# The second half's sum over partitions moved into the first group of direct products, and its squares added from the fourth chunk on

## The chip, the cores and the metric

One NeuronCore of a Trainium2 chip runs the whole program. The metric is device time in microseconds (us), the median of the runs; lower is better. PE is the matmul engine (TensorE), DVE is VectorE, ACT is ScalarE, POOL is GpSimd, SP is SyncE, which issues the loads from HBM.

## The reference

A two-layer backbone on 256 context tokens and 1024 latent tokens, 1024 features each, in fp32. Layer 0 mixes tokens by a gated short convolution, layer 1 by attention; each layer ends in a gated convolutional FFN, and it is the head of the two FFNs that this change touches:

```python
def rmsnorm(x, g):
    xf = x.astype(jnp.float32)
    y = xf * lax.rsqrt(jnp.mean(xf * xf, axis=-1, keepdims=True) + EPS)
    return y.astype(x.dtype) * g
...
def conv_ffn(h, w_up, conv_w, conv_b, w_down):
    u, g = jnp.split(h @ w_up, 2, axis=-1)
    u = dwconv3(u, conv_w, conv_b)
    return (jax.nn.gelu(u) * g) @ w_down
...
    xs = xs + g1s * ys
    hs = modulate(rmsnorm(xs, norm_ffn_g[i]), sh2s, sc2s)
    xs = xs + g2s * conv_ffn(hs, ffn_w_up[i], ffn_conv_w[i], ffn_conv_b[i], ffn_w_down[i])
```

## The kernel before

**Layout.** Features lie on the 128 partitions and tokens along the free dimension, so the activations x are eight chunks x0 to x7 of 128 features. All tokens (with a little padding) are cut into two halves of 644 columns. A matmul operand in fp32 is split into a rounded part and a rest ("hi" and "lo" for weights, "op..h" and "op..l" for activations), and each product is three passes: hi times h, hi times l, lo times h. One pass here is two matmuls of 322 columns, called a pair below.

**The head of an FFN** (function `ffn`). First `half_round` finishes the mixer's output product, for the first half of the tokens and then for the second: eight tiles each, taken out of PSUM into x by DVE (line 802) and stored. The PSUM tiles use three slots in turn, s0, s1, s2, and the direct products after them use the same slots: the first group's three accumulators get the slots that tiles 5, 6 and 7 of the second half held.

The normalisation needs, for each half, the squares of all eight chunks added up (`sq_chunk`: ACT squares a chunk, line 324, and DVE adds it, line 325), their sum over the 128 partitions (`rstd_cols`: two PE matmuls against a matrix of ones, line 336, called psq), and then a reciprocal root (lines 343 to 345 on ACT, 346 to 348 on DVE). `plain(c, half)` multiplies a chunk by it (DVE, line 819), applies scale and shift (ACT, line 822) and splits it (ACT line 827, DVE line 828). The first half's four chunks x0 to x3 become op1 and x4 to x7 op2; the second half's become op4 and op3.

While the second half of `half_round` is still running on PE, `hook(m)` starts the first half's normalisation after tile 2 and calls `prepare_chunk(m - 3)` after each later tile; three more chunks follow after it. Each `prepare_chunk` does one chunk of the first half and adds one chunk's squares for the second half.

**The direct products** (function `direct`, line 880). Two tiles of the u part and two of the gate part are computed without the seven-product scheme that follows. For each half there is a group of three accumulators and a group of one, each over op1 then op2 (second half: op4 then op3). A group is two parts of four steps; one step of the first group is three accumulators times three passes, nine pairs. At the end of the first group of the first half the caller's hook runs: it issues psq for the second half, and the second half's `plain` for all chunks comes after the second group.

**The pairs** (function `pairs`, line 864). The other tiles of W_up go two by two through seven half-size products with operands op1 to op7, in the order 1, 2, 6, 5, 7, 3, 4. `differences` makes op5, op6, op7 and a new op4 on DVE (line 841) and splits them. A pair has three PSUM slots; products 1, 6, 7 and 4 share one, 5 and 3 another. So before product 6, 7, 4 or 3 can start, what the one before it left in the slot must have been read: by ACT copies called c1 (line 947), c2 (line 963) and c3 (line 966), and by DVE additions (line 905). The first pair's stage also holds the convolution of the two direct u tiles (`gated`: ACT line 380, DVE lines 381 and 382, each on 1288 columns, then the gelu on ACT, line 919) and the loads of their gate tiles gl from HBM (line 936, one buffer).

**Weights** come as raw tiles by SP (three buffers), ACT rounds them to hi (line 218), and DVE or POOL makes lo (line 219); there are four hi and four lo buffers, so a hi tile waits until PE is done with the weights four before it.

**What sets the order.** PE and SP follow the order of the code. For DVE, ACT and POOL the order is chosen when the program is built, by a scheduler with its own estimates of time; so a change of code at one place can move instructions of these three engines elsewhere.

Of the kernel before, what the change touches and what calls it, by code (L numbers as in the profile page):

```python
# [20 lines left out]
KD = 8  # L21
# [6 lines left out]
NH = (TX + 4) // 2  # L28
# [35 lines left out]
def backbone(ctx: ExitStack, tc, xT, cpk, ada_w, w_in, w_out, w_qkv, w_oa, w_ob, w_up, w_dn,  # L64
             kctx, vctx, rpb, yT, kT, vT):
    nc = tc.nc
    V, A, G, T = nc.vector, nc.scalar, nc.gpsimd, nc.tensor
# [27 lines left out]
    rstd = const.tile([P, TXX], F32, name="rstd")  # L95
# [130 lines left out]
    def unit():  # L226
        top_up()
        return ready.pop(0)
# [90 lines left out]
    def sq_chunk(sqa, c, o=0, n=TX, eng=None):  # L319
        if c == 0:  # L320
            A.activation(sqa[:, o:o + n], S.x[c][:, o:o + n], AF.Square)
        else:
            sq = S.tp.tile([P, TX + 2], F32, tag=("y", "ub")[c % 2], name="sq")
            A.activation(sq[:, 0:n], S.x[c][:, o:o + n], AF.Square)
            (eng or G).tensor_tensor(out=sqa[:, o:o + n], in0=sqa[:, o:o + n], in1=sq[:, 0:n], op=ALU.add)  # L325
# [450 lines left out]
    def slot(k, nm):  # L776
        return S.ps3.tile([P, 2, 512], F32, tag=f"s{k % 3}", name=nm)
# [34 lines left out]
    def rstd_half(half, tmp=None):  # L812
        for i in range(2):
            rstd_cols(rstd, half * NH + i * NB, NB, i, tmp and tmp[i])

    def scaled(c, half, l, n):

        x, o = S.x[c], half * NH
        V.tensor_tensor(out=x[:, o:o + NH], in0=x[:, o:o + NH], in1=rstd[:, o:o + NH], op=ALU.mult)  # L819
        for r, (a, b) in enumerate(((0, NP_), (S0, NH)) if half == 0 else ((0, 0), (NH, TX))):  # L820
            if b > a:
                A.activation(x[:, a:b], x[:, a:b], AF.Identity, scale=amod[:, n, c, r:r + 1],
                             bias=mod[:, l, 3 * KD + c, r:r + 1])

    def op_split(q, k, src):
        hi, lo = S.ops[q][k]
        A.activation(hi, src, AF.Copy)
        V.tensor_tensor(out=lo, in0=src, in1=hi.bitcast(F32), op=ALU.subtract)
# [5 lines left out]
    def plain(c, half, l, n):  # L834
        scaled(c, half, l, n)
        op_split(PLAIN[half][c // 4], c % 4, S.x[c][:, half * NH:(half + 1) * NH])
# [30 lines left out]
    def direct(half, nm, take, hook=None):  # L867

        n = 1 + 4 * half
        for grp in DIRECT:  # L870
            accs = [slot(n + i, f"{nm}d{half}_{g}_{j}") for i, (g, j) in enumerate(grp)]
            n += len(grp)
            for kh in range(2):
                us = [unit() for _ in grp]
                for k, (bh, bl) in enumerate(S.ops[PLAIN[half][kh]]):
                    w = slice(k * P, (k + 1) * P)
                    for acc, (wh, wl) in zip(accs, us):
                        for pi, (ww, aa) in enumerate(((wh, bh), (wh, bl), (wl, bh))):
                            for b in range(2):
                                T.matmul(acc[:, b, 0:NB], ww[:, w], aa[:, b * NB:(b + 1) * NB],  # L880
                                         start=kh + k + pi == 0, stop=kh == 1 and k == 3 and pi == 2)
            for acc, (g, j) in zip(accs, grp):
                take(half, g, j, acc)
            if hook:
                hook()
                hook = None

    def pairs(n, nm, take, hooks):

# [11 lines left out]
    def ffn(fin, l, gseg, n):  # L901
# [92 lines left out]
        ops_c = [open_ops("opa", (1, 2, 4, 3))]  # L994

        def prepare_chunk(c):
            plain(c, 0, l, n)
            sq_chunk(rstd, c, NH, NH, eng=V)

        def hook(m):  # L1000
            if m == 2:
                rstd_half(0)
            elif m > 2:
                prepare_chunk(m - 3)

        half_round(fin, f"h{l}", l, gseg, hook)
        for c in range(KD - 3, KD):
            prepare_chunk(c)
# [5 lines left out]
        ops_c.append(c)  # L1014
        gates.pop(0)
        direct(0, f"u{l}_", direct_out, lambda: rstd_half(1, [rstd[:, i * NB:(i + 1) * NB] for i in range(2)]))
        for c in range(KD):
            plain(c, 1, l, n)
        direct(1, f"u{l}_", direct_out)
        differences()  # L1020
        close(S.right[2])
# [228 lines left out]
    for rt in range(2):  # L1250
        b = at.tile([P, 3, 640], F32, tag=f"bt{rt}", name=f"bt{rt}", bufs=1)
# [160 lines left out]
    for i in range(NT + 3):  # L1412
        if i < NT:
            h, k = tiles[i][0], i % 10
# [113 lines left out]
```

## Time and profile before

| what | value |
|---|---|
| median of 3 runs | 3104.92 us (3103.65 to 3110.19) |
| the profiled execution | 3106.48 us |
| its span | 3104.7 us |
| PE busy | 3024.6 us, 97% of the span |
| DVE busy | 1542.8 us, 50% |
| ACT busy | 1142.3 us, 37% |
| POOL busy | 839.9 us, 27% |
| granted TensorE clock, mean | 0.992 |

Shares of busy time are averages over stages with different limits. The two FFN heads are the stretches from about 512 to 660 us and from about 2162 to 2311 us of the span. In a timeline row, the first number is the start in us from the span's start, the second how long the row lasted, xN how many instructions it merges, and the bracket how long the engine sat idle before it and what ended that idle time, as far as semaphores tell. A matmul row of one pair lasts 0.45 to 0.46 us at the full granted clock but the next one starts 0.30 us after it, because they are pipelined; at half clock it lasts 0.74 and the next starts 0.54 us after it.

### The profile page before, as it was taken

What the parts mean: (1) busy time and instruction counts of PE and PEld (TensorE: products, weight loads), DVE (VectorE), ACT (ScalarE), POOL (GpSimd) and SP (SyncE); (2) the same over time, 40 slices, a digit from 0 to 9 for tenths busy, and PEclk for the clock granted to TensorE, in tenths of its full rate; (3) what the DMA queues carried; (4) which work ended last, traced back from release to release, by engine and by line L of the source; (5) the groups of instructions that cost most, each with busy time, mean ns of one, the idle gap of its engine ahead of it and who ended that gap; (6) DMA issues with size and microseconds to landing.
All of it is one profiled execution on the core that took longest, in us unless ns stands there. A gap on an engine that the chain in (4) does not pass through costs nothing. (4 is left out here: it accounts for less than half of the span.)

```text
span 3104.7 us, 47013 instructions
## 1 busy us (share of the span) xinstructions
PE 3024.6 (97%) x18765; PEld 2676.1 (86%) x18765; DVE 1542.8 (50%) x2313; ACT 1142.3 (37%) x1886; POOL 839.9 (27%) x767
## 2 busy tenths in 40 slices
PE   8999999899999999999999999999899999999998
PEld 5676788899999988888887888878899999998887
DVE  5432336865444453333455555666784444444335
ACT  4111113743333331124455555553653333422122
POOL 2111121054344331124212212111033443422123
PEclk9999999999999999999999999999899999999999
DMA  6745412232221252223544445566332212144221
GB/s 216 207 142 194 137 57 98 86 102 69 65 79 58 79 202 77 86 74 102 145 129 126 130 133 132 161 195 215 116 108 64 79 59 79 58 160 136 72 79 71
DMA packets 192250, 355.16 MB, mean 114 GB/s; under 512 B 33870, under 2 KB 91470, under 8 KB 192030
## 3 DMA queue, kind: packets, MB, share of 16 engines
q1 hardware_dynamic: 145839, 274.21, 29.6%
q10 hardware_dynamic: 46191, 77.93, 6.8%
q8 instruction: 148, 2.42, 0.3%
q14 instruction: 72, 0.59, 0.1%
HBM read 269.63 MB, written 83.16 MB: 114 GB/s over the span
## 5 line engine op out<-in xcount | busy, mean ns | idle before, releaser
L219 POOL TENSOR_TENSOR lo<-raw,hi 128x512 fp32r<-128x512 f32 x218 | 298.3, 1371 | 1221.0 <-ACT hi L218 1143.7
L218 ACT ACTIVATE hi<-raw 128x512 fp32r<-128x512 f32 x250 | 155.7, 628 | 716.3 <-PE acc_d L284 354.5
L396 DVE SCALAR_TENSOR_TENSOR x<-acc_d,mod,x 128x256 f32<-128x256 f32 x208 | 174.3, 879 | 309.9 <-PE acc_d L284 309.9
L219 POOL TENSOR_TENSOR lo<-raw_a,hi 128x512 fp32r<-128x512 f32 x154 | 204.8, 1330 | 309.1 <-ACT hi L218 309.0
L218 ACT ACTIVATE hi<-raw_a 128x512 fp32r<-128x512 f32 x160 | 100.7, 630 | 327.1 <-PE u L864 185.1
L219 POOL TENSOR_TENSOR lo<-ra_a,hi 128x512 fp32r<-128x512 f32 x80 | 139.1, 1739 | 136.9 <-ACT hi L218 126.1
L1349 ACT ACTIVATE p<-p,ng 128x640 f32<-128x640 f32 x128 | 106.0, 828 | 153.5 <-DVE ng L1347 153.0
L1362 ACT ACTIVATE ptb<-pt 128x256 f32<-128x256 f32 (+1 forms) x288 | 110.1, 421 | 79.8 <-PE pt L1361 73.0
L186 DVE TENSOR_TENSOR s<-ra_a,ra_a 128x512 f32<-128x512 f32 x40 | 43.3, 1082 | 183.4 <-DMA ra_a<-w_up 183.4
L1347 DVE CUSTOM_DVE_ANT_0 p<-sc,bt 128x640 f32<-128x640 f32 x128 | 105.4, 823 | 41.2 <-PE sc L1345 31.6
L284 PE MATMUL a_q<-xh,hi 128*128 128x512 f32 (+1 forms) x456 | 119.5, 367 | 1.4 <-DVE t L1145 0.6
L284 PE MATMUL a_q<-xh,lo 128*128 128x512 f32 (+1 forms) x456 | 117.1, 365 | 0.0
L284 PE MATMUL a_q<-xl,hi 128*128 128x512 f32 (+1 forms) x456 | 116.5, 364 | 0.0
L1361 PE MATMUL pt<-ck,p 128*128 128x128 f32 x704 | 104.7, 273 | 7.2 <-DVE vts L1161 5.8
L1361 PEld LDWEIGHTS pt<-ck,p 128*128 128x128 f32 x704 | 85.4, 140 | 28.2 <-DVE vts L1161 7.2
L1302 POOL TENSOR_TENSOR k<-kd,k 128x512 fp32r<-128x512 f32 x48 | 61.8, 1317 | 166.6 <-ACT k L1301 129.9
L218 ACT ACTIVATE hi<-ra_a 128x512 fp32r<-128x512 f32 x80 | 50.2, 628 | 132.0 <-PE u L864 132.0
L1351 DVE TENSOR_SCALAR p<-p,rc 128x640 f32<-128x640 f32 (+1 forms) x160 | 95.4, 596 | 4.6
L381 DVE SCALAR_TENSOR_TENSOR y<-ub,ck,y 128x1288 f32<-128x1288 f32 x44 | 72.7, 1656 | 48.8 <-ACT y L380 48.8
L284 PE MATMUL acc_d<-fh_f,hi 128*128 128x512 f32 (+1 forms) x384 | 95.4, 357 | 0.4 <-DVE x L396 0.4
L284 PE MATMUL acc_d<-fh_f,lo 128*128 128x512 f32 (+1 forms) x384 | 95.3, 357 | 0.0
L284 PE MATMUL acc_d<-fl_f,hi 128*128 128x512 f32 (+1 forms) x384 | 95.0, 355 | 0.0
(363 smaller groups left out, 8179.2 us busy)
## 6 DMA issues: line engine op xcount, KB each, us to landing
adau<-ada_w SPq DMA_DIRECT2D x80, 512.0 KB, 4.5
fS<-y ACTq DMA_DIRECT2D x44, 642.0 KB, 4.9
fr<-fS SPq DMA_DIRECT2D x44, 642.0 KB, 4.1
raw<-w_dn SPq DMA_DIRECT2D x88, 256.0 KB, 2.7
raw_a<-w_up SPq DMA_DIRECT2D x80, 256.0 KB, 2.7
ra_a<-w_up SPq DMA_DIRECT2D x80, 256.0 KB, 2.9
x<-xS SPq DMA_DIRECT2D x24, 642.0 KB, 6.8
raw<-w_in SPq DMA_DIRECT2D x48, 256.0 KB, 4.2
```

Of the source, the lines that this page charges most:

```text
L186: V.tensor_tensor(out=t["s1"], in0=t["a21"], in1=t["a22"], op=ALU.add)
L218: A.activation(hi, raw, AF.Copy)
L219: (V if i in on_dve else G).tensor_tensor(out=lo, in0=raw, in1=hi.bitcast(F32), op=ALU.subtract)
L284: T.matmul(acc[:, g, 0:nn] if hasattr(acc, "shape") else acc[g][:, 0:nn], ww, aa[:, o:o + nn], start=first and pi == 0, stop=last and pi == 2)
L381: V.scalar_tensor_tensor(out=y, in0=ub[:, 0:n], scalar=w4[:, 0:1], in1=y, op0=ALU.mult, op1=ALU.add)
L396: V.scalar_tensor_tensor(out=xx, in0=a, scalar=mod[:, l, seg * KD + m, r:r + 1], in1=xx, op0=ALU.mult, op1=ALU.add)
L1302: G.tensor_tensor(out=k2[:, o:o + 512], in0=kd[:, o:o + 512], in1=k1.bitcast(F32)[:, o:o + 512], op=ALU.subtract)
L1347: V.tensor_tensor_reduce(out=pp, in0=sc[:, 128:768], in1=btt[rh][:, CT[j], :], scale=1.0, scalar=MASK, op0=ALU.add, op1=ALU.min, accum_out=ng)
L1349: A.activation(pp, pp, AF.Exp, scale=-1.0, bias=ng, accum_out=sm)
L1351: V.tensor_scalar(out=pp, in0=pp, scalar1=rc, scalar2=None, op0=ALU.mult)
L1361: T.transpose(pt[:, e, :], p[:, c * P:(c + 1) * P], ident)
L1362: A.activation(ptb[:, cs[0]:cs[0] + len(cs), :], pt[:, 0:len(cs), :], AF.Copy)
```

## The change

`prepare_chunk` adds no squares for its first three chunks; its calls for x3 to x6 add the squares of x0 to x3, one chunk each, and its call for x7 adds those of x4 to x7. `direct` calls the hook, which issues psq and the reciprocal root of the second half, after the second of the four steps of the first group's second part, no longer after the group.

```diff
                             for b in range(2):
                                 T.matmul(acc[:, b, 0:NB], ww[:, w], aa[:, b * NB:(b + 1) * NB],
                                          start=kh + k + pi == 0, stop=kh == 1 and k == 3 and pi == 2)
+                    if hook and kh == 1 and k == 1:
+                        hook()
+                        hook = None
             for acc, (g, j) in zip(accs, grp):
                 take(half, g, j, acc)
-            if hook:
-                hook()
-                hook = None
...
         def prepare_chunk(c):
+
             plain(c, 0, l, n)
-            sq_chunk(rstd, c, NH, NH, eng=V)
+            for b in range(*((0, 0) if c < 3 else (c - 3, c - 2) if c < KD - 1 else (c - 3, KD))):
+                sq_chunk(rstd, b, NH, NH, eng=V)
```

No instruction is added or taken away on any engine; SP's order is the same. The places below are those of the first FFN; the second shows the same.

DVE where the second half of `half_round` ends, before (x0 to x7 are the chunks, h0_1_5 to h0_1_7 the last three PSUM tiles, sq a chunk's squares):

```order
L819 TENSOR_TENSOR x1_104<-x1_104,rstd_70 128x644
L325 TENSOR_TENSOR rstd_70<-rstd_70,sq_4152 128x644
L802 SCALAR_TENSOR_TENSOR x5_98<-h0_1_5_4155,mod_75,x5_98 128x320 x2
L828 TENSOR_TENSOR op1l_3838<-x0_103,op1h_3837 128x644
L219 TENSOR_TENSOR lo64_4128<-raw64_4125,hi64_4127 128x512
L819 TENSOR_TENSOR x2_105<-x2_105,rstd_70 128x644
L325 TENSOR_TENSOR rstd_70<-rstd_70,sq_4176 128x644
L802 SCALAR_TENSOR_TENSOR x6_99<-h0_1_6_4179,mod_75,x6_99 128x320
L828 TENSOR_TENSOR op1l_3838<-x1_104,op1h_3837 128x644
L802 SCALAR_TENSOR_TENSOR x6_99<-h0_1_6_4179,mod_75,x6_99 128x320
L819 TENSOR_TENSOR x3_106<-x3_106,rstd_70 128x644
L325 TENSOR_TENSOR rstd_70<-rstd_70,sq_4200 128x644
```

The same place now:

```order
L819 TENSOR_TENSOR x1_104<-x1_104,rstd_70 128x644
L802 SCALAR_TENSOR_TENSOR x5_98<-h0_1_5_4151,mod_75,x5_98 128x320 x2
L819 TENSOR_TENSOR x2_105<-x2_105,rstd_70 128x644
L828 TENSOR_TENSOR op1l_3838<-x0_103,op1h_3837 128x644
L219 TENSOR_TENSOR lo64_4127<-raw64_4124,hi64_4126 128x512
L802 SCALAR_TENSOR_TENSOR x6_99<-h0_1_6_4172,mod_75,x6_99 128x320 x2
L819 TENSOR_TENSOR x3_106<-x3_106,rstd_70 128x644
L802 SCALAR_TENSOR_TENSOR x7_96<-h0_1_7_4194,mod_75,x7_96 128x320
L828 TENSOR_TENSOR op1l_3838<-x1_104,op1h_3837 128x644
L802 SCALAR_TENSOR_TENSOR x7_96<-h0_1_7_4194,mod_75,x7_96 128x320
```

Three additions of squares (line 325) no longer stand ahead of the evacuations of the last three tiles. They stand further down, where DVE prepares op2:

```order
L828 TENSOR_TENSOR op2l_3840<-x6_99,op2h_3839 128x644
L325 TENSOR_TENSOR rstd_70<-rstd_70,sq_4239 128x644
L828 TENSOR_TENSOR op2l_3840<-x7_96,op2h_3839 128x644
L325 TENSOR_TENSOR rstd_70<-rstd_70,sq_4242 128x644
L325 TENSOR_TENSOR rstd_70<-rstd_70,sq_4245 128x644
L219 TENSOR_TENSOR lo65_4272<-raw65_4269,hi65_4271 128x512
L325 TENSOR_TENSOR rstd_70<-rstd_70,sq_4248 128x644
L219 TENSOR_TENSOR lo66_4278<-raw66_4275,hi66_4277 128x512
```

Two more of them stand between op2's last split and lo66 than before, when lo65, lo66 and lo67 (the weights of the group's second part) followed that split directly.

ACT in the first pair's stage, before (c2 and c3 are the copies of products 6 and 5, y0_0 and y0_1 the convolved direct tiles):

```order
L963 ACTIVATE c2_0_0_2_4992<-u0_2_1_4900 128x644
L218 ACTIVATE hi84_4999<-ra0_0_2_a22_4761 128x512
L218 ACTIVATE hi85_5031<-raw0_1_2_a11_5029 128x512
L966 ACTIVATE c3_0_0_2_5027<-u0_2_5_4998 128x644
L919 ACT_TABLE_LOAD
L919 ACTIVATE y0_0_4887<-y0_0_4887 128x1288
L919 ACTIVATE y0_1_4895<-y0_1_4895 128x1288
```

And now:

```order
L963 ACTIVATE c2_0_0_2_4992<-u0_2_1_4900 128x644
L218 ACTIVATE hi84_4999<-ra0_0_2_a22_4761 128x512
L919 ACT_TABLE_LOAD
L919 ACTIVATE y0_0_4887<-y0_0_4887 128x1288
L919 ACTIVATE y0_1_4895<-y0_1_4895 128x1288
L966 ACTIVATE c3_0_0_2_5027<-u0_2_5_4998 128x644
```

The copy c3 stood ahead of the table load and the two gelus, and now stands behind them.

## Rows read from the trace of the kernel before

**Rows 1.** The page: the span, and the lines of the chain that ended last.

```profile
span 3104.7 us, 47013 instructions
...
PE u L864 15%; PE acc_d L284 7%; PE acc_f L716 2%; PE u_d L880 2%; PE acc_wob L284 1%; PE h L797 1%; DMA fr<-fS 0%; DVE x L819 0%; DVE x L841 0%; DVE rstd L325 0%; DMA gl<-fS 0%; DVE y L381 0%; PE psq L336 0%; DVE x L396 0%; POOL sqa L325 0
```

**Rows 2.** Timeline of PE, first FFN, direct products of the first half.

```profile
549.60 0.90 PE L880 MATMUL u_d<-op1h,hi 128*128 128x322 f32 x2 [2.89 <-DVE x L802]
...
552.83 0.88 PE L880 MATMUL u_d<-op1h,hi 128*128 128x322 f32 x2 [1.25 <-ACT op1h L827]
...
563.97 0.56 PE L880 MATMUL u_d<-op2h,lo 128*128 128x322 f32 x2
...
566.16 0.45 PE L880 MATMUL u_d<-op2h,hi 128*128 128x322 f32 x2
...
574.18 1.25 PE L336 MATMUL psq<-rstd,ones 128*128 128x322 f32 x4
```

**Rows 3.** Timeline of PE, first FFN, second half's direct products and first two pairs.

```profile
585.17 0.56 PE L880 MATMUL u_d<-op4h,hi 128*128 128x322 f32 x2 [2.59 <-ACT op4h L827]
...
616.14 0.46 PE L864 MATMUL u<-op1h,hi 128*128 128x322 f32 x2
...
634.51 0.46 PE L864 MATMUL u<-op3h,hi 128*128 128x322 f32 x2
...
640.06 0.56 PE L864 MATMUL u<-op4h,hi 128*128 128x322 f32 x2 [1.81 <-DVE ub L905]
...
645.25 0.46 PE L864 MATMUL u<-op1h,hi 128*128 128x322 f32 x2
...
654.25 0.57 PE L864 MATMUL u<-op6h,hi 128*128 128x322 f32 x2 [1.68 <-ACT c L947]
...
658.18 0.46 PE L864 MATMUL u<-op5h,hi 128*128 128x322 f32 x2
```

**Rows 4.** Timeline of DVE, first FFN.

```profile
551.67 1.01 DVE L802 SCALAR_TENSOR_TENSOR x<-h,mod,x 128x320 f32<-128x320 f32 x2
...
561.74 0.83 DVE L325 TENSOR_TENSOR rstd<-rstd,sq 128x644 f32<-128x644 f32 x1 [0.78 <-ACT sq L324]
...
580.89 4.53 DVE L819 TENSOR_TENSOR x<-x,rstd 128x644 f32<-128x644 f32 x6
...
627.48 4.62 DVE L381 SCALAR_TENSOR_TENSOR y<-ub,ck,y 128x1288 f32<-128x1288 f32 x2 [0.41 <-ACT y L380]
632.02 5.10 DVE L382 SCALAR_TENSOR_TENSOR y<-ub,ck,y 128x1288 f32<-128x1288 f32 x2
...
644.96 1.50 DVE L906 TENSOR_TENSOR y<-y,gl 128x1284 f32<-128x1284 f32 x1 [4.22 <-DMA gl<-fS]
```

**Rows 5.** Timeline of ACT, first FFN.

```profile
562.25 1.66 ACT L218 ACTIVATE hi<-raw 128x512 fp32r<-128x512 f32 x3
...
575.11 0.54 ACT L343 ACTIVATE rstd<-psq,epsb 128x322 f32<-128x322 f32 x1
...
631.37 0.69 ACT L966 ACTIVATE c<-u 128x644 f32<-128x644 f32 x1
...
637.16 1.28 ACT L919 ACTIVATE y<-y 128x1288 f32<-128x1288 f32 x1 [1.23 <-DVE y L382]
```

**Rows 6.** Timeline of PE, second FFN: the places of 549.60 and 658.18.

```profile
2199.61 0.91 PE L880 MATMUL u_d<-op1h,hi 128*128 128x322 f32 x2 [2.88 <-DVE x L802]
...
2310.72 0.46 PE L864 MATMUL u<-op5h,hi 128*128 128x322 f32 x2
```

**Rows 7.** Two stretches: us, PE busy (instructions), granted clock, DMA share, GB/s.

```profile
550.00:556.00 6.00, 4.75 (x18) 0.51 0.29 112
...
640.00:646.00 6.00, 5.94 (x30) 0.72 0.97 333
```

**Rows 8.** Timeline of POOL, first FFN, first pair's lo tiles.

```profile
620.64 7.59 POOL L219 TENSOR_TENSOR lo<-ra_a,hi 128x512 fp32r<-128x512 f32 x1 [11.03 <-ACT hi L218]
...
629.45 1.29 POOL L219 TENSOR_TENSOR lo<-raw_a,hi 128x512 fp32r<-128x512 f32 x1 [1.23 <-ACT hi L218]
```

## The prediction

> **What bounds the kernel now.** I read the page first: PE is busy for 97% of the span, and the chain that ended last is nearly all PE [rows 1]. So a change pays only where PE stands still or runs at half clock. Then I read the timeline of PE around the two FFN heads for rows with a bracket, and beside it those of DVE and ACT, to see what each gap waits for. In the first FFN there are five gaps of over one us, 2.89, 1.25, 2.59, 1.81 and 1.68 us [rows 2, 3]. The second FFN has the same places, 1650.01 us later (549.60 against 2199.61) [rows 2, 6].
>
> The first two gaps, at 549.60 and 552.83, are slots. The accumulators there take over the PSUM of the last two tiles of the half round, and DVE empties the last one by the row at 551.67, which ends at 552.68 [rows 4]; the op1h named at 552.83 only ended last by chance. The clock then stood at 0.51 [rows 7]. The third gap, 2.59 us at 585.17, is op4: the second half's normalisation starts from psq at 574.18 [rows 2], ACT's first step on it is at 575.11 [rows 5], the first multiplication at 580.89 [rows 4]. The fourth, at 640.06, is DVE: its addition of c3 stands behind the convolutions, 627.48 to 637.12 [rows 4]. The fifth is ACT's copy of a product, late for the same reason. So from 580.89 on DVE's chain is almost as tight as PE.
>
> **The change part by part.** The pace of PE at full clock is (574.18 - 566.16) / 27 pairs = 0.297 us a pair [rows 2], so a step of nine pairs is 2.67 us.
>
> *The squares, moved down.* With three additions less in front (each 0.74 us from start to start), DVE empties tile 7 by about 549.8, not 552.68. PE could then be through op1 some 3 us earlier. But the same work now comes later: ACT has two squares between op2's last split and hi65, and DVE two additions between op2l and lo65 and one between lo65 and lo66. Adding up the two queues from 542 on, hi65 ends at 561.7 (ACT reached it at 562.25 before [rows 5]) and lo65 at about 562.95, while PE took the first lo pass at 563.97 before [rows 2]. lo66 and lo67 end at 564.3 and 564.9. So the second step of that part starts at about 565.2 instead of 566.16: **1.0 us** is gained, and the rest of the slot gap turns into a wait for weights. That wait, 1 to 2 us from 560 on, may draw half clock; I take it that it doesn't, since the gap of 1.81 us at 640.06 drew only part of one, a mean of 0.72 in that stretch [rows 7], and keep the other case for the range: a stretch at half clock costs what the second half's direct products show, 616.14 - 585.17 = 30.97 us for 96 pairs that take 28.51 at full pace, so **2.45 us** [rows 3].
>
> *psq, moved up.* Its two halves cost PE the same 0.84 us at either place. They now start at 565.2 + 2.67 = 567.9, 6.3 us earlier than at 574.18. From psq to the first multiplication took 6.71 us before, with four lo tiles of DVE and copies of ACT in between; the order now has neither in the chain, so about 5.4, and the multiplication starts at 573.3, **7.6 us earlier** than 580.89 [rows 4]. ACT's evictions of the first group and hi72 still stand before op4h, but these wait for PE, so op4h and op4l of x0 are ready at about 581, when PE arrives: 565.2 + 2.67 + 0.84 + 2 x 2.67 for the group, and 7.13 for the single accumulator's 24 pairs, is 581.2. Before it was 585.17. So the op4 gap goes, 4.0 us with the 1.0 above, and its half clock, 2.45: the pairs start at 581.2 + 28.5 = 609.7 instead of 616.14, **6.4 us** gained. Split tiles op3 and lo73 to lo75 come within 0.5 us of need, by the same adding up.
>
> *What is late next: c3.* DVE's work from 573.3 to the convolutions is that of before plus the four lo tiles that now fall into it (2.4 us), less idle time of about 2. So the convolutions start 7.2 us earlier, at 620.3, and end at 629.9. But ACT's copy c3 now stands behind both gelus. Before, it ran at 631.37, ahead of the gelu at 637.16 [rows 5]. Now it must wait for the second gelu, which waits for the second convolution: 629.9 + 1.3 + 0.7 = 631.9. Product 3 reuses c3's slot, and PE would want to start it 18.37 us after the first pair (634.51 - 616.14 [rows 3]), less the 0.2 us it lost there, at 627.9. **A new gap of 4.0 us** takes back most of it: product 3 starts at 631.9 against 634.51. Behind it on PE is everything; on DVE the addition of c3 and the load of the next gl. After the gaps of 2.89 and 2.59 us PE ran at half clock [rows 2, 3, 7], so product 3 costs 3.56 + 2.45 = 6.0, and product 4 starts at 637.9. Its old gap is gone, since the addition of c3 is done by then. Product 4 ends, and the second pair starts, at 641.5, where it started at 645.25, itself after 1.6 us lost at a clock of 0.72 (5.19 us for 12 pairs of 3.56) [rows 3, 7]: **3.8 us** gained.
>
> *The second pair.* The order puts its c1 copy ahead of the next gelu, and the weight differences ahead of the next convolutions; DVE's multiplication by the second gl stands before an addition that the next eviction needs, and gl can land at 637.8 (issued 7.2 us earlier than now, 644.96 before [rows 4]). The sum along ACT puts c1 at about 646.6 to 647.3, PE wants it at 641.5 + 7.1 = 648.6. So the gap at 654.25 goes: 654.25 - 648.6 = **5.6 us** for the first FFN. From there on PE has no gap of that size in the FFN, and the gain stays.
>
> *The second FFN* has the same instructions. Before, its fifth gap was longer: product 5 of the second pair is at 2310.72, and 658.18 + 1650.01 is 2308.19, so 2.5 us more are there to be gained [rows 3, 6]: **8.1 us**.
>
> **Sum.** 5.6 + 8.1 = 13.7 us. The profiled execution took 3106.48 us, 1.56 above the median and 1.78 above its own span; 3106.5 - 13.7 = 3092.8, or **3091.2** against the median of 3104.92.
>
> **The rivals.** *More is kept.* If the gap before product 3 draws no half clock, or is shorter than 4 us since DVE's chain runs ahead of my adding up, the gain is 1.4 us more in each FFN (then c1 binds) up to some 3.5 us: 3084 to 3088. The row at 640.06 speaks for it, a gap of 1.81 us with part of a half-clock stretch after it; the length of 4 us speaks against.
>
> *Half clock twice.* If the wait for hi65 draws half clock too, everything up to the convolutions is 2.1 to 2.45 us later in each FFN, and the gain is about 9 us: 3096.
>
> *POOL holds the first pair.* The lo tile for product 7 took 7.59 us beside DVE's splits, and the one after it 1.29 [rows 8]. If the convolutions hold POOL back in the same way, product 7 or 3 waits until 629.9 + 1.3 = 631.2 or later for its weights, not only for c3, and product 3 starts near 634: the gain is 3.4 in the first FFN and 6 in the second at full pace, some 5 in all with half clock: 3100, no measurable change. Against it: POOL's row at 629.45 ran at 1.29 us beside a convolution, and the long one should have ended by 621. The Trainium skill (GPSIMD Engine Reference, 1. Specifications) says that GpSimd shares its SBUF interfaces with VectorE and contends with DVE instructions in a 2-port mode or with two SBUF inputs; the convolutions have two SBUF inputs, so by that sentence alone this rival would be the rule, and the time about 3100. The row at 629.45 disagrees with its strict reading.
>
> *The change doesn't reach its end.* psq comes earlier, but op4 waits for ACT behind evictions that PE releases, and the op4 gap stays: then only 1.0 us of the first part is left, 3103.
>
> *Slower: c3 behind the gelus.* The mechanism is the new place of c3 on ACT, its price is PE's wait for the second convolution. If DVE loses its lead of 7.2 us in the 28 us of the second half's direct products, where it waits for hi tiles that PE frees, and 3 us more, the convolutions end at 640, c3 at 642 and product 3 starts 7.6 us later than at 634.51; with half clock, less the old gap and its clock (3.4) and the fifth gap (1.7 to 4.2), each FFN is 3 to 5 us slower: 3113. It decides from an end of the convolutions at about 637. Against it: the work is the same and starts 7 us earlier.
>
> **How the numbers follow.** The forecast with all between 9 and 17 us gained: 0.53. More is kept (17 to 21): 0.11. Half clock twice, and other ways to 6 to 9 us: 0.14. POOL, op4 still late, or other ways to within 6 us: 0.17. Slower: 0.05. A measurement of this kernel can tell about 0.2%, 6.2 us, from no change; so faster 0.78, same 0.17, slower 0.05. The range that leaves out the slower case, part of the no-change cases and the top of the best one goes from 3085 to 3101.
>
> **What would show it.** After the change PE should have no gap before op4, DVE's first multiplication with the second half's root about 7 us nearer to the head than now, psq between two steps of the first group, and a new gap of about 4 us before product 3 of the first pair, ended by c3. The gap before product 4 should be gone. If op4 still has its gap, my walk along ACT is wrong; if product 3 has none, the DVE chain is; if PE stands at half clock between 561 and 567, the weights at lo65 cost more than I took. A result above 3101 means that c3 or POOL took back the gain.

## The result, and the profile after

The changed kernel took 3088.53 us (median of 4 runs, 3084.79 to 3095.62), the kernel before beside it 3106.88 us: a ratio of **0.9944**, 95% interval 0.9922 to 0.9965, so 11 to 24 us less. In two later sessions it took 3093.27 us (0.9955, 0.9942 to 0.9969) and 3091.46 us (0.9952, 0.994 to 0.9964). The forecast was 3091.2 us, 13.7 us less; the three medians are 18.35, 13.69 and 15.49 us less. The first of these lies among the gains that the prediction gave to its rival "more is kept" (17 to 21 us), the other two among those of the forecast (9 to 17).

The page of the kernel after, its span (3104.7 before, [rows 1]). The page counts ten instructions more in all, but none more on the four engines: PE has 18765, DVE 2313, ACT 1886 and POOL 767 in both kernels.

```profile
span 3085.8 us, 47023 instructions
```

Timeline of PE of the kernel after, first FFN: the places of [rows 2, 3]. The columns are the start and length in us, engine, line, operation, tiles, count, and in brackets the idle time before it and what ended that:

```profile
549.72 0.53 PE L880 MATMUL u_d<-op1h,hi 128*128 128x322 f32 x2 [1.33 <-DVE x L802]
...
561.58 0.67 PE L880 MATMUL u_d<-op2h,hi 128*128 128x322 f32 x2 [2.67 <-ACT hi L218]
...
566.25 0.46 PE L880 MATMUL u_d<-op2h,hi 128*128 128x322 f32 x2
...
568.91 1.25 PE L336 MATMUL psq<-rstd,ones 128*128 128x322 f32 x4
...
582.53 0.46 PE L880 MATMUL u_d<-op4h,hi 128*128 128x322 f32 x2
...
611.12 0.46 PE L864 MATMUL u<-op1h,hi 128*128 128x322 f32 x2
...
631.14 0.57 PE L864 MATMUL u<-op3h,hi 128*128 128x322 f32 x2 [1.97 <-ACT c L966]
...
638.41 0.46 PE L864 MATMUL u<-op1h,hi 128*128 128x322 f32 x2
...
647.30 0.57 PE L864 MATMUL u<-op6h,hi 128*128 128x322 f32 x2 [1.58 <-ACT c L947]
...
650.98 0.46 PE L864 MATMUL u<-op5h,hi 128*128 128x322 f32 x2
```

The slot gap of 2.89 us is 1.33 us, and a new gap of 2.67 us stands before the group's second part (op2), waiting for its first hi tile. The expectations and the text below call this place *the second step*; the row at 566.25 is the second of that part's four steps, and psq runs behind it, 5.27 us earlier than at 574.18. The gap before op4 is gone, the pairs start 5.02 us earlier, and product 3 has a new gap ended by c3. The gap before product 6 of the second pair is still there. Product 5 behind it, the last of the marks, is 7.20 us earlier.

Timeline of DVE and ACT of the kernel after, first FFN: the places of [rows 4, 5].

```profile
574.07 0.83 DVE L819 TENSOR_TENSOR x<-x,rstd 128x644 f32<-128x644 f32 x1
...
620.58 4.62 DVE L381 SCALAR_TENSOR_TENSOR y<-ub,ck,y 128x1288 f32<-128x1288 f32 x2 [0.41 <-ACT y L380]
625.13 4.06 DVE L382 SCALAR_TENSOR_TENSOR y<-ub,ck,y 128x1288 f32<-128x1288 f32 x2
...
637.00 1.50 DVE L906 TENSOR_TENSOR y<-y,gl 128x1284 f32<-128x1284 f32 x1 [4.93 <-DMA gl<-fS]
```

```profile
629.22 1.28 ACT L919 ACTIVATE y<-y 128x1288 f32<-128x1288 f32 x1 [0.19 <-DVE y L382]
630.40 0.69 ACT L966 ACTIVATE c<-u 128x644 f32<-128x644 f32 x1
```

From the first multiplication on, DVE hardly stands still. Its busy time in two stretches of 10 us (columns: stretch, length, DVE busy and instructions, granted clock, DMA share, GB/s), first of the kernel after, then of the kernel before:

```profile
584.00:594.00 10.00, 10.00 (x15) 1.00 0.08 33
594.00:604.00 10.00, 9.82 (x15) 1.00 0.51 159
```

```profile
591.00:601.00 10.00, 8.62 (x13) 1.00 0.26 69
601.00:611.00 10.00, 8.84 (x14) 1.00 0.25 93
```

Before, it lost 2.54 us in the two at the same distance behind its first multiplication, now 0.18, so the convolutions come when DVE's queue reaches them. PE is busy for all 20 us of the same stretches too, so busy time alone does not say which of the two engines sets the pace; e9 and e10 below do. Behind the convolutions stands a chain that crosses every engine. SP's queue, DVE, ACT and POOL of the kernel after, from the end of the convolutions (629.19) to product 6 (647.30); the rows of a queue give the issue:

```profile
631.36 0.33 SPq L936 DMA_DIRECT2D gl<-fS  x1
631.73 0.42 SPq L165 DMA_DIRECT2D raw_a<-w_up  x1
632.20 1.40 SPq L165 DMA_DIRECT2D ra_a<-w_up  x2
```

```profile
641.03 0.69 DVE L192 TENSOR_TENSOR raw_a<-s,raw_a 128x512 f32<-128x512 f32 x1
...
642.42 1.55 DVE L381 SCALAR_TENSOR_TENSOR y<-ub,ck,y 128x1288 f32<-128x1288 f32 x1
644.01 2.47 DVE L382 SCALAR_TENSOR_TENSOR y<-ub,ck,y 128x1288 f32<-128x1288 f32 x1
```

```profile
642.53 2.59 POOL L219 TENSOR_TENSOR lo<-raw_a,hi 128x512 fp32r<-128x512 f32 x1 [2.84 <-ACT hi L218]
645.07 0.10 POOL L751 MEMSET ub<- 128x4 f32 x1
```

```profile
645.20 1.46 ACT L380 ACTIVATE y<-ub,ck 128x1288 f32<-128x1288 f32 x1 [1.64 <-POOL ub L751]
646.57 0.68 ACT L947 ACTIVATE c<-u 128x644 f32<-128x644 f32 x1
```

The load of the second gl is issued when the first gating multiplication has freed its tile, and the weight loads stand behind it on SP. gl lands at 637.00, the weight differences follow the second multiplication on DVE, then hi, then POOL's lo, behind which the zero pads of ub wait, then L380, then c1, then product 6. That lo tile took 2.59 us where others take 1.29, beside the L381 that had started 0.11 us before it.

The second FFN after, PE [rows 6]:

```profile
2292.19 0.56 PE L864 MATMUL u<-op6h,hi 128*128 128x322 f32 x2 [1.47 <-ACT c L947]
...
2295.87 0.46 PE L864 MATMUL u<-op5h,hi 128*128 128x322 f32 x2
```

One place differs there: the second step waited 0.50 us and not 2.67, since PE came to it later, behind a stretch at half clock in the group's first part (granted clock 0.56 from 2195 to 2201). Counted from the first half's psq it still started at the same point, 28.39 us against 28.42; so it is hi on ACT that sets this place.

Where the 18.9 us of the span went: measured from the first half's psq (533.31 before, 533.16 after; 2183.34 and 2178.88) to product 5, the FFNs took 124.87 and 127.38 us before, 117.82 and 116.99 after: **7.05 and 10.39 us**. In the first FFN the 7.05 us are 5.12 to psq, 1.63 from there to the convolutions and 1.03 within them, less 0.98 from their end to product 6, and 0.25 from there to product 5; in the second they are 6.35, 2.20, 1.06, less 0.97, and 1.75. Between product 5 and the next psq, where nothing is changed, the kernel after lost 2.74 us; 0.15 lies ahead, and 4.05 us behind the last mark. That middle stretch took 1525.16 to 1532.73 us in the fourteen profiles of this study: a single profile can mislead by that much, so what follows is read from the two FFN stretches and from medians together.

### The profile page after: what moved, and what is told of

It reads as the page before. It is cut to its first block, busy times and chain, and to the rows that moved or that the text cites. A ratio compares the mean times of both kernels' runs of the same rounds, so it can differ in the third digit from the quotient of the medians.

```text
span 3085.8 us, 47023 instructions
## 1 busy us (share of the span) xinstructions
PE 3014.7 (98%) x18765; PEld 2668.5 (86%) x18765; DVE 1539.9 (50%) x2313; ACT 1142.2 (37%) x1886; POOL 834.5 (27%) x767
## 5 line engine op out<-in xcount | busy, mean ns | idle before, releaser
L219 POOL TENSOR_TENSOR lo<-ra_a,hi 128x512 fp32r<-128x512 f32 x80 | 130.8, 1635 | 144.3 <-ACT hi L218 144.3
L381 DVE SCALAR_TENSOR_TENSOR y<-ub,ck,y 128x1288 f32<-128x1288 f32 x44 | 73.1, 1664 | 49.2 <-ACT y L380 49.2
```

Source lines behind the costliest of these rows:

```text
L219: (V if i in on_dve else G).tensor_tensor(out=lo, in0=raw, in1=hi.bitcast(F32), op=ALU.subtract)
L381: V.scalar_tensor_tensor(out=y, in0=ub[:, 0:n], scalar=w4[:, 0:1], in1=y, op0=ALU.mult, op1=ALU.add)
```

## The experiments

The theory after the result: the gain is the moved sum, and what the squares give at the slots the second step takes back. A second one grew out of the runs: **DVE, not PE, carries the time from psq to the second pair.** This table has both. The times are of the first FFN; "conv" is the first L381 and the end of the second L382; the last column is both FFN stretches added (first half's psq to product 5).

| kernel | median us | ratio to before, 95% | psq | conv from psq | conv end | product 6 from conv end | FFNs, us |
|---|---|---|---|---|---|---|---|
| before | 3106.9 | 1 | 574.18 | 53.30 | 637.12 | 17.13 | 252.25 |
| changed | 3088.53 | 0.9944 (0.9922 to 0.9965) | 568.91 | 51.67 | 629.19 | 18.11 | 234.81 |
| changed again | 3093.27 | 0.9955 (0.9942 to 0.9969) | 569.92 | 51.68 | 630.20 | 18.19 | 237.44 |
| changed, third | 3091.46 | 0.9952 (0.994 to 0.9964) | 569.27 | 51.55 | 629.43 | 18.41 | 236.40 |
| e1 squares only | 3106.39 | 1.0001 (0.9993 to 1.001) | 574.47 | 53.64 | 637.75 | 17.07 | 252.29 |
| e2 sum only | 3088.21 | 0.9945 (0.9932 to 0.9957) | 568.59 | 51.74 | 628.94 | 18.38 | 236.94 |
| e3 c3 first | 3091.55 | 0.9946 (0.9932 to 0.996) | 568.87 | 51.63 | 629.10 | 17.39 | 238.09 |
| e4 gate later | 3088.04 | 0.9939 (0.9925 to 0.9952) | 568.99 | 51.64 | 629.22 | 17.91 | 235.18 |
| e5 both | 3090.81 | 0.9948 (0.9935 to 0.9961) | 568.46 | 51.56 | 628.63 | 17.69 | 236.56 |
| e6 squares behind | 3086.22 | 0.9935 (0.9923 to 0.9948) | 568.36 | 51.55 | 628.51 | 18.38 | 232.34 |
| e8 behind, gate | 3084.38 | 0.9928 (0.9915 to 0.9941) | 568.18 | 51.72 | 628.49 | 18.37 | 231.22 |
| e9 four behind | 3092.20 | 0.995 (0.9937 to 0.9963) | 570.29 | 51.99 | 631.93 | 16.29 | 237.46 |
| e10 sum one later | 3106.45 | 1.0 (0.9992 to 1.0009) | 571.32 | 52.01 | 632.98 | 18.57 | 251.75 |
| e11 sum one earlier | 3093.89 | 0.9956 (0.9943 to 0.9968) | 566.54 | 53.20 | 628.34 | 19.52 | 235.86 |

The changed kernel was run twice more as it is, beside the others.

> The changed kernel as it is, to stand beside the parts on the same chip: 14 to 20 us under the kernel before by every theory.

> The changed kernel as it is, to stand beside these on the same chip: 3088 to 3093 us by every theory, 13 to 19 us under the kernel before.

Measured: 13.69 and 15.49 us under the kernel before; the first is just below the lower end of its expectation (14).

### One part each: e1 and e2

The squares alone (the sum goes back behind the group):

```diff
-                    if hook and kh == 1 and k == 1:
-                        hook()
-                        hook = None
             for acc, (g, j) in zip(accs, grp):
                 take(half, g, j, acc)
+            if hook:
+                hook()
+                hook = None
```

> The squares are moved as in the changed kernel, the sum over partitions stands behind the first group of direct products again. Theory (the gain comes from the sum over partitions standing earlier): the gaps of 2.89 and 1.25 us at the first direct products shrink to some 1.3 us and less, the wait for the second step's first weights (2.67 us) takes most of that, the sum over partitions runs at about 573 us in the first FFN, and the gap of 2.6 us ahead of the first op4 with its half clock stays: 1 to 3 us under the kernel before in all. Rival (the squares are what held the engines): 6 us or more under it, so half of the changed kernel's gain or more without the moved sum. Second rival: without the moved sum the wait of 2.67 us is pure loss, and the time is 1 to 4 us over the kernel before.

The sum alone (a square per chunk, as before):

```diff
-            for b in range(*((0, 0) if c < 3 else (c - 3, c - 2) if c < KD - 1 else (c - 3, KD))):
-                sq_chunk(rstd, b, NH, NH, eng=V)
+            sq_chunk(rstd, c, NH, NH, eng=V)
```

> The sum over partitions is moved as in the changed kernel, the squares stay one per chunk as before. Theory: the gap of 2.89 us at the first direct products stays and that of 2.67 us at the second step is not there, so the sum over partitions runs at 568 to 570 us, as in the changed kernel (568.91), the gap ahead of op4 is gone, and the time is 14 to 18 us under the kernel before, within 3 us of the changed kernel. Rival (both parts are needed): less than 9 us under it, since the sum over partitions would wait for the squares or the slot gaps would cost 3 us per FFN against the changed kernel.

PE of e1, then of e2, first FFN:

```profile
585.47 0.56 PE L880 MATMUL u_d<-op4h,hi 128*128 128x322 f32 x2 [2.60 <-ACT op4h L827]
```

```profile
549.35 0.91 PE L880 MATMUL u_d<-op1h,hi 128*128 128x322 f32 x2 [2.88 <-DVE x L802]
```

The squares alone change nothing: 3106.39 us against 3106.96, a ratio of 1.0001, and op4 waits 2.60 us as before. The sum alone gives 18.75 us, on the same chip where the whole change gave 13.69; its FFNs took 236.94 us, the changed kernel's three profiles 234.81 to 237.44. Its psq runs at 568.59 with the slot gap of 2.88 us untouched. So the gain is the sum's place, and the squares' move adds nothing that shows. e1's expectation of 1 to 3 us less was a little too high. What these runs do not part is the place of the sum from the orders on DVE, ACT and POOL that come with it: the 1.03 us within the convolutions, for instance, come from fewer lo tiles of POOL beside L382 (last section).

### Product 3's wait and product 6's wait: e3, e4, e5

e3 calls the gelus of the two direct tiles later, so that c3 comes between them on ACT:

```diff
         for j in range(2):
-            gated(j)
+            gated(j, False)
...
         def direct_gate(j):
+            A.activation(ys[j], ys[j], AF.Gelu_apprx_tanh)
...
-              {(NDIR, 6): lambda: direct_gate(0), (NDIR, 7): lambda: direct_gate(1)})
+              {(NDIR, 5): lambda: direct_gate(0), (NDIR, 7): lambda: direct_gate(1)})
```

(gated's new argument leaves out the gelu, which direct_gate now calls.)

> The changed kernel, with the gelus of the two direct tiles called behind product 5 and product 7 of the first pair, so that on ScalarE the copy c3 stands between them and not behind both. Theory (product 3's wait of 1.97 us for c3 sets nothing, since product 6 of the second pair waits later for the chain that starts at the load of the second gate tile): product 3's wait falls under 0.8 us, product 6's grows by as much or more, and the time stays within 3 us of the changed kernel's 3088 to 3093. Rival (the wait for c3 is a loss of its own): product 6's wait stays at 1.6 us and the time is 3 to 5 us under the changed kernel's.

e4 calls the second gating behind product 4; e5 is e3 and e4 together:

```diff
-              {(NDIR, 6): lambda: direct_gate(0), (NDIR, 7): lambda: direct_gate(1)})
+              {(NDIR, 6): lambda: direct_gate(0), (NDIR, 4): lambda: direct_gate(1)})
```

> The changed kernel, with the second direct tile's gating called behind product 4 instead of product 7, so that the weight differences and the sums of the pair stand ahead of that multiplication on VectorE, which waited 4.93 us for its load. Theory (that wait on VectorE is what ends product 6's wait of 1.58 us in the second pair): the convolution of the pair's first tile starts some 2 us earlier, product 6's wait falls under 1 us, and the time is 1 to 4 us under the changed kernel's. Rival (the copy c1, now behind the gelu of the same pair on ScalarE, is the later one): product 6's wait stays over 1.5 us and the time is the changed kernel's or up to 6 us over it.

> The changed kernel with both of the two edits before: the copy c3 between the gelus, and the second gating behind product 4. Theory: with VectorE's wait out of the way the earlier product 3 is kept, so product 3's wait is under 0.8 us, product 6's under 1.6 us, and the time is 3 to 6 us under the changed kernel's. Rival: product 6 takes it all, and the time is within 3 us of the changed kernel's.

PE of e3, first FFN:

```profile
629.59 0.57 PE L864 MATMUL u<-op3h,hi 128*128 128x322 f32 x2 [0.46 <-ACT c L968]
...
646.49 0.56 PE L864 MATMUL u<-op6h,hi 128*128 128x322 f32 x2 [1.87 <-ACT c L949]
```

SP's queue, DVE and PE of e4, first FFN:

```profile
620.62 1.11 SPq L165 DMA_DIRECT2D ra_a<-w_up  x2
...
632.00 0.33 SPq L936 DMA_DIRECT2D gl<-fS  x1
```

```profile
637.60 2.41 DVE L906 TENSOR_TENSOR y<-y,gl 128x1284 f32<-128x1284 f32 x1 [0.17 <-DMA gl<-fS]
```

```profile
647.13 0.46 PE L864 MATMUL u<-op6h,hi 128*128 128x322 f32 x2
```

In e3 product 3 starts 1.55 us earlier than in the changed kernel, and none of it is kept at product 5, which is at 651.88 against 650.98. Half of it still shows at product 6 (646.49 against 647.30); that waits 1.87 us, and the half clock behind the wait takes the rest, 5.39 us to product 5 instead of 3.68. The time is the changed kernel's, as the theory had it; its step that product 6's wait would grow by as much did not come (1.58 to 1.87 us). So that product 3's wait sets nothing is the likelier reading, but not shown apart from the half clock. In e4 the ra_a weights are issued at 620.62 instead of 632.20, ahead of the gl load; DVE's wait of 4.93 us is 0.17, and product 6 waits for nothing in the first FFN and 0.83 us in the second. That much of the chain is shown. In time it is 3088.04 us, 0.5 us under the lowest of the changed kernel's three medians (3088.53 to 3093.27), so a gain is not shown. In the first FFN product 3's wait (1.94 us) was followed by the half clock, which ate the difference; in the second it was not, and that FFN took 117.17 us against 116.99. e5 (3090.81 us) missed its 3 to 6 us: with product 3 early, product 6 waits again (2.04 and 1.71 us), now for a c1 that stands behind a gelu, as its rival had it.

### The wait at the second step: e6, e8, e9

e6 puts the squares of chunks 5 to 7 behind the fetch of the second step's weights:

```diff
-            for b in range(*((0, 0) if c < 3 else (c - 3, c - 2) if c < KD - 1 else (c - 3, KD))):
+            for b in range(*((0, 0) if c < 3 else (c - 3, c - 2) if c < KD - 1 else (c - 3, c - 2))):
...
+        def last_squares():
+            for b in range(KD - 3, KD):
+                sq = tmp("c1", f"sq{l}_{b}", 2)
+                A.activation(sq, S.x[b][:, NH:2 * NH], AF.Square)
+                add(rstd[:, NH:2 * NH], rstd[:, NH:2 * NH], sq)
...
                 us = [unit() for _ in grp]
+                if pre and kh == 1:
+                    pre()
+                    pre = None
```

(pre is a new argument of direct, last_squares for the first half.)

> The changed kernel, with the squares of chunks 5 to 7 behind the fetch of the second step's weights on ScalarE and VectorE. Theory (the wait of 2.67 us for hi at the second step, with the half clock behind it, is the two squares that stand ahead of it on ScalarE): that gap falls under 1 us, no half clock follows, the sum over partitions runs 2 to 4 us earlier than 568.91, and the time is 3 to 8 us under the changed kernel's if the products keep the lead, of which the wait ahead of product 6 may take 1 to 2 us per FFN. Rival (the weights are late themselves, or the squares then hold back the sum over partitions): the gap stays or comes back at the sum, and the time is within 2 us of the changed kernel's.

e8 is e6 and e4 together; e9 is e8 with `KD - 4` for `KD - 3`, chunk 4's square taken out of the chunks too, and the sum behind chunk 2 of the step (`k == 2`).

> The last three squares behind the fetch of the second step's weights, and the second gating behind product 4. In the kernel with the squares alone behind, product 3's wait of 1.85 us was followed by the half clock and product 6 then waited 0.34 us. Theory: what the gating gives back adds to the squares only where product 6 waits, so the time is 0 to 3 us under that kernel's 3086.2. Rival (the copy c1 behind a gelu): product 6 waits over 1.5 us and the time is 1 to 6 us over it.

> As the kernel with three squares behind and the later gating (3084.38), with the squares of chunks 4 to 7 behind the second step's weights and the sum over partitions one chunk later in that step, since its last squares now stand behind a weight that waits for its load. Theory: the wait at the second step (1.41 us) falls under 0.9 us, the sum over partitions stands at about 569 us, op4 still comes without a wait, and the time is 0 to 3 us under 3084. Rival (the slack ahead of op4, 2.6 us by the profile of the changed kernel, is used up): a gap of 0.5 to 2 us ahead of op4 with the half clock behind it, and the time is 2 to 6 us over 3084.

PE of e6, then of e9, first FFN:

```profile
560.92 0.56 PE L883 MATMUL u_d<-op2h,hi 128*128 128x322 f32 x2 [1.41 <-ACT hi L218]
```

```profile
561.55 0.56 PE L883 MATMUL u_d<-op2h,hi 128*128 128x322 f32 x2
...
582.14 0.46 PE L883 MATMUL u_d<-op4h,hi 128*128 128x322 f32 x2
...
648.22 0.90 PE L864 MATMUL u<-op6h,hi 128*128 128x322 f32 x2 [3.74 <-ACT c L950]
```

From the first half's psq, e6 starts the second step 1.23 us sooner than the changed kernel (27.19 us against 28.42) and psq 1.12 us sooner (34.63 against 35.75). The wait fell to 1.41 us, not under 1, since the split of chunk 7 still stands ahead of hi, half clock still followed it in the first FFN, and psq did not come the 2 to 4 us sooner of the theory. Only its time came as expected: 7.05 us under the changed kernel beside it. The two intervals just overlap; the FFN stretches (232.34 us against 234.81 to 237.44) point the same way, but account for 2.5 to 5.1 us of it. e8 is the fastest kernel of the study, 3084.38 us, 22.4 us under the kernel before and within its theory's 0 to 3 us under 3086.2; that it beats e6 is not shown. e9 removed the wait at the second step altogether, as expected, and op4 came without one, yet it took 3092.20 us, outside both of its expectations. Counted from the first half's psq (which itself ran 2.1 us later here), the sum stands where e8 has it (34.63 us against 34.61) and PE starts the pairs 1.75 us sooner; but the convolutions end 1.35 us later, since both L382 now run beside lo tiles of POOL (5.10 us for the two, not 4.06), c1 stands behind a gelu, and product 6 waits 3.74 us with half clock behind it. PE came sooner and gained nothing.

### Where the sum stands: e10 and e11

e10 is the changed kernel with the sum one chunk later (`k == 2`), e11 is e2 with it one chunk earlier (`k == 0`).

> The changed kernel with the sum over partitions one chunk later in the second step, about 2.7 us. In the kernel before, op4 came 11.0 us after the sum (585.17 less 574.18); with the sum at 568.91 that is 579.9, and TensorE reached op4 at 582.53, so 2.6 us lie idle in between. Theory: the shift uses that up, op4 comes with no gap or one under 0.5 us and the time is within 4 us of the changed kernel's. Rival (each microsecond that the sum stands earlier is gained): 2.7 us per FFN lost, with a gap ahead of op4 and the half clock, so 6 to 10 us over the changed kernel's.

> The kernel with the moved sum alone (squares one per chunk as before, 3088.21), and the sum one chunk earlier still, at about 566 us. Theory (once op4 comes without a wait, an earlier sum gives nothing on TensorE, and what follows is bound by the first pair's convolutions and the gating): within 3 us of 3088. Rival: the convolutions start earlier too, and product 3's wait of 2.04 us and product 6's of 1.85 us shrink: 3 to 6 us under 3088.

PE of e10, first FFN, then DVE and ACT:

```profile
583.19 0.46 PE L880 MATMUL u_d<-op4h,hi 128*128 128x322 f32 x2
...
611.78 0.46 PE L864 MATMUL u<-op1h,hi 128*128 128x322 f32 x2
...
651.55 0.57 PE L864 MATMUL u<-op6h,hi 128*128 128x322 f32 x2 [1.33 <-ACT hi L218]
```

```profile
627.88 5.10 DVE L382 SCALAR_TENSOR_TENSOR y<-ub,ck,y 128x1288 f32<-128x1288 f32 x2
```

```profile
649.71 1.28 ACT L919 ACTIVATE y<-y 128x1288 f32<-128x1288 f32 x1 [3.34 <-DVE y L382]
650.89 0.61 ACT L218 ACTIVATE hi<-raw_a 128x512 fp32r<-128x512 f32 x1
```

This run felled the theory as far as it spoke of op4. op4 has no gap, the pairs start 0.66 us later than in the changed kernel, and still the whole gain is gone: 3106.45 us, a ratio of 1.0. What is late is DVE. Counted from the first half's psq, the sum is 2.77 us later than in the changed kernel (38.52 us against 35.75), the convolutions start 3.11 us later (90.53 against 87.42) and end 4.15 us later (100.18 against 96.03). Of these 4.15 us 2.77 are the sum, 0.34 the way from it to the convolutions, and 1.04 the lo tiles of POOL that now stand beside both L382 (5.10 us for the two, not 4.06). Another 2.78 us come from the order on ACT that the shift brought with it: a hi tile of the second pair now stands behind both of its gelus, so product 6 waits for the end of its own pair's convolutions (0.46 us more from the end of the first pair's), and takes 6.00 us to product 5 where 3.68 are usual. Together they are the 6.93 us that the first FFN lost. So of the sum's own place the run shows 2.77 us in the first FFN; most of the rest is the order. Neither expectation held: the gap ahead of op4 did not come, and the loss, 15 us against the changed kernel beside it, is over the rival's 6 to 10.

e11 shows the other side. ACT and PE, first FFN:

```profile
645.96 1.26 ACT L919 ACTIVATE y<-y 128x1288 f32<-128x1288 f32 x1
647.12 0.69 ACT L947 ACTIVATE c<-u 128x644 f32<-128x644 f32 x1
```

```profile
647.86 0.56 PE L864 MATMUL u<-op6h,hi 128*128 128x322 f32 x2 [2.97 <-ACT c L947]
```

Counted from the first half's psq, the sum runs 2.22 us earlier than in e2 (33.34 us against 35.56), the convolutions end only 0.77 us earlier (95.14 against 95.91), and c1 stands behind a gelu that costs it 1.16 us (645.96 to 647.12). Nothing is gained: 3093.89 us against e2's 3088.21, with intervals that overlap, and FFN stretches of 235.86 us against 236.94; both expectations were too low. The first multiplication came 2.06 us earlier (571.68 against 573.74), but from 592 to 602 DVE stood still for 1.38 us, waiting for hi tiles and a load; so the pace is DVE's only as long as it has work.

## Why the prediction was right, step by step

*The sum.* 13.7 us were forecast, 13.7 to 18.4 were measured, of which the two FFN stretches of the changed kernel's three profiles show 14.8 to 17.4. The sign and the size rest on psq, and e2 shows that alone it gives the whole.

*The squares.* 1.0 us was to be kept: the second of the part's four steps was put at 565.2, where it had been at 566.16. It started at 566.25, and the worth of this part was nothing (e1). The term that failed is the half clock: I took none behind the wait at the part's first step, and it came. The stretches there and at product 3, columns as in [rows 7]:

```profile
558.00:564.00 6.00, 3.07 (x14) 0.82 0.00 2
564.00:570.00 6.00, 6.00 (x35) 0.89 0.55 174
...
628.00:634.00 6.00, 4.03 (x27) 1.00 0.27 64
```

So psq was at 568.91, not 567.9. The half clock that I had set behind product 3 did not fall there in this profile. The two errors have opposite signs, 1.0 us against 2.45.

*op4 and the pairs.* The gap went, as forecast; the pairs start at 611.12 (forecast 609.7), 5.02 us earlier instead of 6.4. The prediction did not let the gain hang on this: its product 3 follows from the end of the convolutions, and the gap before it takes most of the 6.4 us back. e10 bears that out, which has no gap before op4 either and no gain.

*The convolutions* were put at 620.3 to 629.9 and ran from 620.58 to 629.19. This was the best step, and it is the one on which the time hangs: the prediction called DVE's chain almost as tight as PE, followed it as far as product 3, and counted along PE from there. By the page PE is busy for 98% of the span and DVE for 50%; in the stretches from 584 to 604 DVE is busy for 19.82 of 20 us and PE for all 20. In e9 PE came to the pairs 1.75 us sooner than in e8, in e10 0.66 us later than in the changed kernel; in both the convolutions ended later, and so did the FFN. The Trainium skill (Perfetto Trace Analysis, Optimization Strategy) says that a kernel may have several regimes, with another most-contended engine in each. e9 and e10 agree; the busy shares alone do not show it.

*Product 3.* A gap of 4.0 us with half clock, 2.45 us, product 3 at 631.9, was forecast; it was 1.97 us without, at 631.14. The mechanism was as told, c3 behind the second gelu. The size was off because PE arrived at 629.17, not at 627.9, and the convolutions ended 0.7 us sooner; L382 took 4.06 us where it took 5.10 [rows 4].

*The second pair.* Its start was put at 641.5 and was 638.41; c1 was put at 646.6 to 647.3 and ran from 646.57 to 647.25. But PE wanted it at 645.72, not 648.6, so the gap before product 6, which was to go, stayed (1.58 us). Part of the good figure is luck: PE came 2.9 us sooner than forecast, mostly since the half clock stayed away, and the wait that was not forecast took 1.58 of them back. That c1 was met to 0.1 us is in part luck too: between the landing of gl (637.8 forecast, 637.00 measured) and c1 the prediction shows no terms, and it does not name POOL's lo and the zero pads behind it. That c1 sets this point, which the rival "more is kept" named, is what happened: 7.05 us in the first FFN where 5.6 were forecast, 10.39 where 8.1 were.

*The rivals.* POOL did not hold the first pair: its lo tiles ran 1.29 and 2.54 us beside the convolutions, and product 7 had no gap. In the second pair POOL's lo of 2.59 us at 642.53 is on the path. The Trainium skill (GPSIMD Engine Reference, 1. Specifications) says that a VectorE instruction with two SBUF inputs contends with GpSimd. The rows agree. The prediction held POOL's 1.29 us at 629.45 [rows 8] against that sentence, but the step of DVE beside that lo tile paid: it took 2.59 us, and another of its kind 1.55. DVE of the kernel before:

```profile
629.51 2.59 DVE L381 SCALAR_TENSOR_TENSOR y<-ub,ck,y 128x1288 f32<-128x1288 f32 x1
...
646.38 1.55 DVE L381 SCALAR_TENSOR_TENSOR y<-ub,ck,y 128x1288 f32<-128x1288 f32 x1
```

"Half clock twice" did not come in the first profile, where it came once in each FFN, earlier than thought; in the second FFN of the two later profiles it came behind product 3 as well. c3 behind the gelus did not make the kernel slower, since the convolutions ended at 629.19, far from the 637 from which it decides.

## What to carry to other kernels

When two engines are close to bound, find which of them the moved work feeds, and follow its chain to the far end: here it was 50.6 to 53.8 us from psq to the convolutions and 16.3 to 19.5 us from their end to product 6 in every kernel and both FFNs, while the gap on PE that the change closed did not decide the time. A change of place also changes what an automatic order puts on the other queues 60 us later; one chunk of shift lost the whole gain (e10), in the first FFN 2.77 of 6.93 us by the shift itself and most of the rest by lo tiles beside the convolutions and a hi tile behind two gelus. Undo each half of a two-part change: one half did all of it here.

## What the hardware showed that was not expected

A wait of the same length at the same place did or did not draw the half clock, in the same program. In the second FFN product 3 waited 1.85 us in all three profiles of the changed kernel: in the first one product 4 followed after 3.67 us (2276.15 to 2279.82), in the other two after 5.20 us (2283.41 to 2288.61, and 2279.02 to 2284.22), the same twelve pairs of matmuls at half clock for part of the way. In the first FFN it was 1.97 us with a clock of 1.00 in the changed kernel and 1.85 us with 0.75 in e6 (628 to 634). Of the fourteen waits of 1.85 to 2.08 us before product 3 in these profiles, six were followed by half clock; of the nine of 2.66 or 2.67 us at the second step, all were. The runs do not settle what decides it. A forecast can give a stretch behind such a shorter wait, some 1.5 us here, a chance, but not count on it.

DVE's convolution step L382 took 1.55 us while POOL stood still (e10, at 648.12), and a lo tile of POOL 1.30 us while DVE stood still (changed kernel, at 632.48). Side by side, the one that started second paid for both. In the changed kernel L381 at 642.42 kept its 1.55 us and the lo tile that started 0.11 us behind it took 2.59; L382 at 644.01, with that lo tile still running, took 2.47. In the kernel before the lo tile at 629.45 kept its 1.29 us and L381, 0.06 us behind it, took 2.59. In these three the second ended 1.1 to 1.4 us after the first. Where the two records start 0.02 us apart the order cannot be read from them: L382 at 649.00 took 2.67 us and the lo tile at 649.02 1.29. So the end of a convolution depends on which lo tiles the order puts beside it, and which start first: 4.06 us for two steps in the changed kernel, 5.10 before and in e9 and e10.
